# Row variances of a 64 MB tensor: TensorE's share given to VectorE and ScalarE, in tiles of 16 columns

## The chip, the core and the metric

The kernel runs on one core of a Trainium2 chip. The metric is the device time of one execution in microseconds (us), the median of several runs. Profiles are of one execution each.

## What is computed

```python
# x: (32, 512, 1024) float32
mean_sq = np.mean(x**2, axis=-1)
sq_mean = np.mean(x, axis=-1)**2
return mean_sq - sq_mean          # (32, 512): the variance of each row
```

There are 16384 rows of 1024 numbers, 67.1 MB to read and 64 KB to write.

## The kernel before

The rows are laid out so that partition p holds rows 128p to 128p+127. A *column* i is one row on each of the 128 partitions: a 128x1024 block of 512 KB. There are 128 columns, and each needs its mean and its mean square.

Three ways of doing a column share the work:

- **bn** (`do_bn_col`, L109): VectorE reads the two halves of the row with `bn_stats` (L112) and joins them with `bn_aggr` (L115). That gives mean and variance at once.
- **Square with a sum** (`do_square_col`, L117): ScalarE squares the row and sums it (L118, an ACTIVATE followed by a read of the accumulator), which gives the mean square. The plain sum then comes from another place: a `reduce_sum` of VectorE (L171, L206), a Copy pass of ScalarE with a sum (L213), or TensorE.
- **TensorE sums** (`do_tensor_cols`, L126): eight transposes of 128x128 (L133) add up in PSUM, VectorE copies the folded block to SBUF (L142), a matmul with ones sums it (L143), and VectorE copies the sums out (L152).

The columns 0 to 103 are loaded in 13 tiles of 8 columns (32 KB per partition, 4 MB each, L165), in three buffers. In each tile three columns are bn columns, two are Square plus `reduce_sum`, three are Square plus TensorE. The eight columns 120 to 127 are loaded first of all (L79) into a buffer of their own, and one of them is done with each of the tiles 2 to 9. The columns 104 to 119 come last, in seven loads of 4, 4, 2, 2, 2, 1 and 1 columns (L195), into a buffer of 64 KB per partition that nothing else uses. They are done in a pattern of four: Square plus `reduce_sum`, Square plus Copy, bn, bn.

`combine` (L81) forms mean square less squared mean for the columns that are not bn columns: a small Square on ScalarE (L83) and a subtraction on VectorE (L90, L102). It is called for the first 64 columns, the eight early ones, and the next 40. The results of the columns 0 to 103 are stored from ScalarE's queue (L189), beside the last loads. At the end the last 24 columns are joined (L221, L230) and stored from SP's queue (L237).

All loads stand on SP's queue in program order. A load into a buffer that was used before waits on SP for the engines that read it. Each engine runs its instructions in program order. Every ACTIVATE waits for the one ahead of it on ScalarE, since all write the same scratch tile.

Of the kernel before, what the change touches and what calls it, by code (L numbers as in the profile page):

```python
# [3 lines left out]

# [4 lines left out]


# [1 line left out]
def kernel(  # L13
# [2 lines left out]
    x: bass.AP,  # L16
    out: bass.AP,
):
    nc = tc.nc
    P = nc.NUM_PARTITIONS  # L20
    FP32 = mybir.dt.float32

    xf = x.flatten_outer_dims()
    N, D = xf.shape
    assert N % P == 0
    ntiles = N // P
    DCH = D // P

    def col_range(c0, n):
        return dataclasses.replace(  # L30
            xf,
            offset=c0 * D,
            ap=[[ntiles * D, P], [D, n], [1, D]],
        )

    out_ji = dataclasses.replace(out, offset=0, ap=[[ntiles, P], [1, ntiles]])

    FMAX = nc.vector.BN_STATS_FMAX
    nsub = (D + FMAX - 1) // FMAX

    inv_sqrt_d = 1.0 / math.sqrt(D)

    NBODY = 13
    END0 = NBODY * 8
    FILL0 = 120

    end_plan = [
        (104, 4),
        (108, 4),
        (112, 2),  # L50
        (114, 2),
        (116, 2),
        (118, 1),
        (119, 1),
    ]

    xpool = ctx.enter_context(tc.tile_pool(name="xpool", bufs=3))
    spool = ctx.enter_context(tc.tile_pool(name="spool", bufs=8))
    fpool = ctx.enter_context(tc.tile_pool(name="fpool", bufs=4))
    scpool = ctx.enter_context(tc.tile_pool(name="scpool", bufs=2))  # L60
    opool = ctx.enter_context(tc.tile_pool(name="opool", bufs=1))
    ppool = ctx.enter_context(tc.tile_pool(name="ppool", bufs=5, space=bass.MemoryType.PSUM))
    pspool = ctx.enter_context(tc.tile_pool(name="pspool", bufs=2, space=bass.MemoryType.PSUM))

    ident = opool.tile([P, P], FP32)
    masks.make_identity(nc, ident)
    ones = opool.tile([P, 1], FP32)
    nc.gpsimd.memset(ones, 1.0)

    pair_stage = opool.tile([P, 2, ntiles], FP32)  # L70
    msq_stage = opool.tile([P, ntiles], FP32)
    sqm_stage = opool.tile([P, ntiles], FP32)

    scratch = scpool.tile([P, D], mybir.dt.bfloat16)

    xt_end = opool.tile([P, FILL0 - END0, D], FP32)
    xt_fill = opool.tile([P, ntiles - FILL0, D], FP32)

    nc.sync.dma_start(out=xt_fill, in_=col_range(FILL0, ntiles - FILL0))  # L79

    def combine(c0, ngrp, gsize, nbn):  # L81
        n = ngrp * gsize
        nc.scalar.activation(  # L83
            out=sqm_stage[:, c0 : c0 + n],
            in_=pair_stage[:, 0, c0 : c0 + n],
            func=mybir.ActivationFunctionType.Square,
            scale=1.0 / D,
        )
        if nbn == 0:
            nc.vector.tensor_tensor(  # L90
                out=pair_stage[:, 1, c0 : c0 + n],
                in0=msq_stage[:, c0 : c0 + n],
                in1=sqm_stage[:, c0 : c0 + n],
                op=mybir.AluOpType.subtract,
            )
        else:
            var_v = pair_stage[:, 1, c0 : c0 + n].rearrange(
                "p (g k) -> p g k", k=gsize
            )
            msq_v = msq_stage[:, c0 : c0 + n].rearrange("p (g k) -> p g k", k=gsize)  # L100
            sqm_v = sqm_stage[:, c0 : c0 + n].rearrange("p (g k) -> p g k", k=gsize)
            nc.vector.tensor_tensor(  # L102
                out=var_v[:, :, nbn:gsize],
                in0=msq_v[:, :, nbn:gsize],
                in1=sqm_v[:, :, nbn:gsize],
                op=mybir.AluOpType.subtract,
            )

    def do_bn_col(xcol, i):  # L109
        stats = spool.tile([P, nsub, 6], FP32, name="stats")  # L110
        for s in range(nsub):
            nc.vector.bn_stats(  # L112
                out=stats[:, s, :], in_=xcol[:, s * FMAX : (s + 1) * FMAX]
            )
        nc.vector.bn_aggr(out=pair_stage[:, :, i], in_=stats)  # L115

    def do_square_col(xcol, i):  # L117
        nc.scalar.activation(  # L118
            out=scratch,
            in_=xcol,  # L120
            func=mybir.ActivationFunctionType.Square,
            scale=inv_sqrt_d,
            accum_out=msq_stage[:, i : i + 1],
        )

    def do_tensor_cols(xt, cols):  # L126
        if not cols:
            return
        psum_s = pspool.tile([P, 8], FP32, name="psum_s")
        for slot, (k, i) in enumerate(cols):  # L130
            psum_f = ppool.tile([P, P], FP32, name="psum_f")
            for ch in range(DCH):
                nc.tensor.matmul(  # L133
                    out=psum_f,
                    lhsT=xt[:, k, ch * P : (ch + 1) * P],
                    rhs=ident,
                    is_transpose=True,
                    start=(ch == 0),
                    stop=(ch == DCH - 1),
                )  # L140
            folded = fpool.tile([P, P], FP32, name="folded")
            nc.vector.tensor_copy(out=folded, in_=psum_f)  # L142
            nc.tensor.matmul(  # L143
                out=psum_s[:, slot : slot + 1],
                lhsT=folded,
                rhs=ones,
                start=True,
                stop=True,
            )
        i0 = cols[0][1]  # L150
        nt = len(cols)
        nc.vector.tensor_copy(  # L152
            out=pair_stage[:, 0, i0 : i0 + nt], in_=psum_s[:, :nt]
        )

    def do_filler_col(j):
        i = FILL0 + j
        do_square_col(xt_fill[:, j, :], i)
        do_tensor_cols(xt_fill, [(j, i)])

    for gi in range(NBODY):
        c0 = gi * 8
        nbn, ncl = 3, 2
        xt = xpool.tile([P, 8, D], FP32, name="xt")
        nc.sync.dma_start(out=xt, in_=col_range(c0, 8))  # L165

        for k in range(nbn):
            do_bn_col(xt[:, k, :], c0 + k)
        for k in range(nbn, 8):
            do_square_col(xt[:, k, :], c0 + k)  # L170
        nc.vector.reduce_sum(  # L171
            out=pair_stage[:, 0, c0 + nbn : c0 + nbn + ncl],
            in_=xt[:, nbn : nbn + ncl, :],
            axis=mybir.AxisListType.X,
        )
        do_tensor_cols(
            xt, [(k, c0 + k) for k in range(nbn + ncl, 8)]
        )

        if 2 <= gi <= 9:  # L180
            do_filler_col(gi - 2)

        if gi == 7:
            combine(0, 8, 8, 3)
        elif gi == 10:
            combine(120, 1, 8, 0)
        elif gi == 12:
            combine(64, 5, 8, 3)
            nc.scalar.dma_start(  # L189
                out=out_ji[:, 0:END0], in_=pair_stage[:, 1, 0:END0]  # L190
            )

    for (c0, ncols) in end_plan:
        off = c0 - END0
        nc.sync.dma_start(  # L195
            out=xt_end[:, off : off + ncols, :], in_=col_range(c0, ncols)
        )
        for k in range(ncols):
            i = c0 + k
            mode = "CSAA"[(i - END0) % 4]  # L200
            xcol = xt_end[:, off + k, :]
            if mode == "A":
                do_bn_col(xcol, i)
            elif mode == "C":
                do_square_col(xcol, i)
                nc.vector.reduce_sum(  # L206
                    out=pair_stage[:, 0, i : i + 1],
                    in_=xcol,
                    axis=mybir.AxisListType.X,
                )  # L210
            else:
                do_square_col(xcol, i)
                nc.scalar.activation(  # L213
                    out=scratch,
                    in_=xcol,
                    func=mybir.ActivationFunctionType.Copy,
                    accum_out=pair_stage[:, 0, i : i + 1],
                )

    n_end = ntiles - END0  # L220
    nc.scalar.activation(  # L221
        out=sqm_stage[:, END0:ntiles],
        in_=pair_stage[:, 0, END0:ntiles],
        func=mybir.ActivationFunctionType.Square,
        scale=1.0 / D,
    )
    var_v = pair_stage[:, 1, END0:ntiles].rearrange("p (g k) -> p g k", k=4)
    msq_v = msq_stage[:, END0:ntiles].rearrange("p (g k) -> p g k", k=4)
    sqm_v = sqm_stage[:, END0:ntiles].rearrange("p (g k) -> p g k", k=4)
    nc.vector.tensor_tensor(  # L230
        out=var_v[:, :, 0:2],
        in0=msq_v[:, :, 0:2],
        in1=sqm_v[:, :, 0:2],
        op=mybir.AluOpType.subtract,
    )

    nc.sync.dma_start(  # L237
        out=out_ji[:, END0:ntiles], in_=pair_stage[:, 1, END0:ntiles]
    )


# [1 line left out]
_INS = ['x']  # L243
_OUTS = [((32, 512), 'float32')]


# [23 lines left out]
```

## Time and profile before

| What | Value |
|---|---|
| time, median of 3 runs | 167.7 us (167.53 to 167.71) |
| span of the profiled execution, first to last instruction | 165.9 us |
| VectorE (DVE) busy | 107.0 us (64%), 230 instructions |
| ScalarE (ACT) busy | 99.7 us (60%), 175 instructions |
| TensorE (PE) busy, matmuls | 82.8 us (50%), 470 instructions |
| loads on SP's queue (q1) | 67.12 MB, 94.7% of the 16 DMA engines' span |
| mean rate over the span | 405 GB/s |

The span is the time between the first and the last instruction of the profiled execution. The runs' times also take in what lies around it; the page gives no separate time for the profiled execution, so its span is set beside the median of the runs, 1.8 us above it.

A page of this profile cuts the span in 40 equal slices and gives each engine's busy share in tenths. The chain that ended last is followed back from the last instruction, at each step to what released it. A timeline line gives start, length, engine, line and operation.

### The profile page before, as it was taken

The numbers are of one execution on the slowest core, as the hardware profiler recorded it, in microseconds if no ns is written. First come the engines' busy times: TensorE is split into PE (matmuls) and PEld (weight loads), VectorE is DVE, ScalarE is ACT, GpSimd is POOL, SyncE is SP. The second block draws the span as 40 slices with busy tenths as digits, with TensorE's granted clock in tenths as the row PEclk, the third lists the DMA queues.
The fourth block names the chain that finished last, engine by engine and source line by source line (L and its number), as shares of the span: only waits on it lengthen the run. The fifth ranks groups of instructions, "written<-read, shape, count | busy, mean of one in ns | idle before, by whom it ended". The sixth has DMA issues, their size and how long they took to land.

```text
span 165.9 us, 1460 instructions
## 1 busy us (share of the span) xinstructions
PE 82.8 (50%) x470; PEld 78.6 (47%) x470; DVE 107.0 (64%) x230; ACT 99.7 (60%) x175; POOL 0.7 (0%) x7
## 2 busy tenths in 40 slices
PE   0000047293791957749497774929565391950000
PEld 0000046292780947749396764829464381930000
DVE  0000049295791967949396794939769393999993
ACT  3000049093790967939396694939767391998981
POOL 1000000000000000000000000000000000000000
PEclk9999999658576597865858598795978658585555
DMA  5999999999999999999999999999999999999930
GB/s 190 443 427 450 411 450 411 443 443 427 450 399 450 421 435 435 421 443 411 443 423 443 427 435 435 419 450 415 435 435 419 443 421 399 435 417 417 412 140 3
DMA packets 3320, 67.26 MB, mean 405 GB/s; under 512 B 625, under 2 KB 625, under 8 KB 881
## 3 DMA queue, kind: packets, MB, share of 16 engines
q1 hardware_dynamic: 3168, 67.12, 94.7%
q8 instruction: 3, 0.05, 0.1%
q10 hardware_dynamic: 144, 0.05, 0.1%
q14 instruction: 5, 0.03, 0.1%
HBM read 67.11 MB, written 0.07 MB: 405 GB/s over the span
## 4 chain that ended last, share of the span: by engine, by line
DMA 69%; DVE 28%; issue 0%; SPq 0%; ACT 0%; ACTq 0%
DMA xt<-in_x_dram 69%; DVE stats L112 16%; DVE pair_stage L171 7%; DVE pair_stage L206 3%; DVE pair_stage L115 2%; DVE folded L142 0%; SPq L79 0%; ACT sqm_stage L221 0%; SPq L165 0%; DVE pair_stage L230 0%; DVE pair_stage L102 0%; DVE pair_stage L152 0%; ACTq L221 0%
## 5 line engine op out<-in xcount | busy, mean ns | idle before, releaser
L118 ACT ACTIVATE scratch<-xt 128x1024 bf16<-128x1024 f32 x65 | 68.7, 1057 | 59.6 <-DMA xt<-in_x_dram 57.9
L133 PE MATMUL psum_f<-ident,xt 128*128 128x128 f32 x312 | 62.9, 392 | 53.9 <-DMA xt<-in_x_dram 53.9
L133 PEld LDWEIGHTS psum_f<-ident,xt 128*128 128x128 f32 x312 | 59.1, 212 | 54.9 <-DMA xt<-in_x_dram 31.8
L112 DVE BATCH_NORM_STATS2 stats<-xt 128x6 f32<-128x512 f32 x78 | 48.8, 667 | 50.5 <-DMA xt<-in_x_dram 50.5
L171 DVE TENSOR_REDUCE pair_stage<-xt 128x2 f32<-128x2048 f32 x13 | 29.5, 2270 | 0.0
L143 PEld LDWEIGHTS psum_s<-ones,folded 128*128 128x128 f32 x94 | 11.5, 191 | 14.6 <-DVE folded L142 14.6
L143 PE MATMUL psum_s<-ones,folded 128*128 128x1 f32 x94 | 12.5, 252 | 11.4 <-DVE folded L142 11.4
L118 ACT ACTIVATION_READ_ACCUMULATOR scratch<-xt 128x1 f32 x65 | 12.1, 186 | 0.0
L112 DVE BATCH_NORM_STATS2 stats<-xt_end 128x6 f32<-128x512 f32 x16 | 10.1, 666 | 0.0
L142 DVE COPY folded<-psum_f 128x128 f32<-128x128 f32 x47 | 9.8, 267 | 0.0
L115 DVE BATCH_NORM_AGGREGATE pair_stage<-stats 128x2 f32<-128x12 f32 x47 | 9.2, 197 | 0.1
L118 ACT ACTIVATE scratch<-xt_end 128x1024 bf16<-128x1024 f32 x8 | 8.5, 1056 | 1.1 <-DMA xt_end<-in_x_dram 0.9
L133 PE MATMUL psum_f<-ident,xt_fill 128*128 128x128 f32 x64 | 9.0, 286 | 0.0
L118 ACT ACTIVATE scratch<-xt_fill 128x1024 bf16<-128x1024 f32 x8 | 8.5, 1057 | 0.3
L133 PEld LDWEIGHTS psum_f<-ident,xt_fill 128*128 128x128 f32 x64 | 8.2, 155 | 0.0
L152 DVE COPY pair_stage<-psum_s 128x3 f32<-128x3 f32 (+1 forms) x21 | 3.3, 159 | 5.2 <-PE psum_s L143 4.7
L206 DVE TENSOR_REDUCE pair_stage<-xt_end 128x1 f32<-128x1024 f32 x4 | 4.7, 1185 | 0.0
L213 ACT ACTIVATE scratch<-xt_end 128x1024 bf16<-128x1024 f32 x4 | 4.2, 1056 | 0.1
L118 ACT ACT_TABLE_LOAD x1 | 1.3, 1283 | 0.7 <-PEq L254 0.7
L118 ACT ACTIVATION_READ_ACCUMULATOR scratch<-xt_end 128x1 f32 x8 | 1.5, 186 | 0.0
L118 ACT ACTIVATION_READ_ACCUMULATOR scratch<-xt_fill 128x1 f32 x8 | 1.5, 186 | 0.0
L83 ACT ACTIVATE sqm_stage<-pair_stage 128x64 f32<-128x64 f32 (+2 forms) x3 | 0.7, 228 | 0.7 <-DVE pair_stage L152 0.7
(12 smaller groups left out, 2.7 us busy)
## 6 DMA issues: line engine op xcount, KB each, us to landing
xt<-in_x_dram SPq DMA_DIRECT2D x13, 4096.0 KB, 23.1
xt_fill<-in_x_dram SPq DMA_DIRECT2D x1, 4096.0 KB, 12.6
xt_end<-in_x_dram SPq DMA_DIRECT2D x2, 2048.0 KB, 29.8
xt_end<-in_x_dram SPq DMA_DIRECT2D x3, 1024.0 KB, 36.1
xt_end<-in_x_dram SPq DMA_DIRECT2D x2, 512.0 KB, 24.1
out_dram<-pair_stage ACTq DMA_DIRECT2D x1, 52.0 KB, 6.8
out_dram<-pair_stage SPq DMA_DIRECT2D x1, 12.0 KB, 1.4
```

The lines of the kernel that those rows point to most:

```text
L83: nc.scalar.activation(out=sqm_stage[:, c0 : c0 + n], in_=pair_stage[:, 0, c0 : c0 + n], func=mybir.ActivationFunctionType.Square, scale=1 ...
L112: nc.vector.bn_stats(out=stats[:, s, :], in_=xcol[:, s * FMAX : (s + 1) * FMAX])
L115: nc.vector.bn_aggr(out=pair_stage[:, :, i], in_=stats)
L118: nc.scalar.activation(out=scratch, in_=xcol, func=mybir.ActivationFunctionType.Square, scale=inv_sqrt_d, accum_out=msq_stage[:, i : i + 1],)
L133: nc.tensor.matmul(out=psum_f, lhsT=xt[:, k, ch * P : (ch + 1) * P], rhs=ident, is_transpose=True, start=(ch == 0), stop=(ch == DCH - 1),)
L142: nc.vector.tensor_copy(out=folded, in_=psum_f)
L143: nc.tensor.matmul(out=psum_s[:, slot : slot + 1], lhsT=folded, rhs=ones, start=True, stop=True,)
L152: nc.vector.tensor_copy(out=pair_stage[:, 0, i0 : i0 + nt], in_=psum_s[:, :nt])
L171: nc.vector.reduce_sum(out=pair_stage[:, 0, c0 + nbn : c0 + nbn + ncl], in_=xt[:, nbn : nbn + ncl, :], axis=mybir.AxisListType.X,)
L206: nc.vector.reduce_sum(out=pair_stage[:, 0, i : i + 1], in_=xcol, axis=mybir.AxisListType.X,)
L213: nc.scalar.activation(out=scratch, in_=xcol, func=mybir.ActivationFunctionType.Copy, accum_out=pair_stage[:, 0, i : i + 1],)
```

## The change

TensorE, PSUM, `combine`, the early eight columns and the early store are dropped. The 128 columns are cut into eight tiles of 16 columns (64 KB per partition, 8 MB), in three buffers. A string for each tile says who does a column:

- **D**: a bn column on VectorE, two `bn_stats` (L53) and a `bn_aggr` (L56), as before.
- **A**: two passes of ScalarE. A Copy with a scale and a sum (L68) gives the negative mean times 1/sqrt(D) in `neg_mean`; a Square with a scale and `neg_mean` as its bias, with a sum (L76), gives the variance. Of the columns of one load, all Copy passes come ahead of all Square passes.

The tiles 0 to 5 are one load each, with 6 A and 10 D columns. Tile 6 is loaded in 10 and 6 columns, with 4 and 2 A columns among them. Tile 7 is loaded in 5, 3, 2, 1, 1, 1 and 1 columns, with 2, 1, 1, 0, 1, 0 and 1 A columns; its last two columns are loaded in halves of 512 numbers, each read by a `bn_stats` of its own. All loads stand on SP's queue (L34). One store of 64 KB (L105) on SP's queue ends the kernel.

```diff
-    NBODY = 13
-    END0 = NBODY * 8
-    FILL0 = 120
...
+    GROUP = 16
+    NGROUPS = ncols // GROUP
+    LOADS = [[GROUP]] * (NGROUPS - 2) + [[10, 6], [5, 3, 2, 1, 1, 1, 1]]
+    WHO = ["ADDADDADDADADDAD"] * (NGROUPS - 2) + ["ADDADDADADADDADD", "ADDADDADDADADA"]
...
+    def act_cols(cols):
+        s = D ** -0.5
+        for xcol, c in cols:
+            nc.scalar.activation(
+                out=junk,
+                in_=xcol,
+                func=ACTF.Copy,
+                scale=-s / D,
+                accum_out=neg_mean[:, c : c + 1],
+            )
+        for xcol, c in cols:
+            nc.scalar.activation(
+                out=junk,
+                in_=xcol,
+                func=ACTF.Square,
+                scale=s,
+                bias=neg_mean[:, c : c + 1],
+                accum_out=mv[:, 1, c : c + 1],
+            )
+    for g in range(NGROUPS):
+        c0 = g * GROUP
+        xt = xpool.tile([P, GROUP, D], FP32, name="xt")
+        k = 0
+        for n in LOADS[g]:
+            load(xt[:, k : k + n, :] if n > 1 else xt[:, k, :], c0 + k, n)
+            mine = range(k, k + n)
+            act_cols([(xt[:, j, :], c0 + j) for j in mine if WHO[g][j] == "A"])
+            for j in mine:
+                if WHO[g][j] == "D":
+                    dve_col(xt[:, j, :], c0 + j)
+            k += n
+        for j in range(k, GROUP):
+            stats = spool.tile([P, 2, 6], FP32, name="stats")
+            for h in range(2):
+                xh = xt[:, j, h * H : (h + 1) * H]
+                load(xh, c0 + j, 1, h * H, H)
+                dve_half(stats, h, xh)
+            dve_done(stats, c0 + j)
+    nc.sync.dma_start(
+        out=dataclasses.replace(out, offset=0, ap=[[ncols, P], [1, ncols]]),
+        in_=mv[:, 1, :],
+    )
```

More of the change, by code (lines that the diff above doesn't have):

```diff
@@ L2 @@
 import dataclasses
-import math
 from contextlib import ExitStack
@@ L7 @@
 import concourse.tile as tile
-from concourse import bass_utils, masks, mybir
+from concourse import mybir
 from concourse._compat import with_exitstack
@@ L21 @@
     FP32 = mybir.dt.float32
+    ACTF = mybir.ActivationFunctionType
     xf = x.flatten_outer_dims()
@@ L25 @@
     assert N % P == 0
[L26 to L33, printed above, removed]
-        )
[L36 to L41, printed above, removed]
-    NBODY = 13
-    END0 = NBODY * 8
-    FILL0 = 120
[L47 to L55, printed above, removed]
+    ncols = N // P
@@ L57, with load @@
+    H = D // 2
+    def load(dst, c0, n, f0=0, f=D):
+        ap = [[ncols * D, P], [D, n], [1, f]] if n > 1 else [[ncols * D, P], [1, f]]
+        nc.sync.dma_start(
+            out=dst, in_=dataclasses.replace(xf, offset=c0 * D + f0, ap=ap)
+        )
+    GROUP = 16
+    NGROUPS = ncols // GROUP
+    LOADS = [[GROUP]] * (NGROUPS - 2) + [[10, 6], [5, 3, 2, 1, 1, 1, 1]]
+    WHO = ["ADDADDADDADADDAD"] * (NGROUPS - 2) + ["ADDADDADADADDADD", "ADDADDADADDADA"]
     xpool = ctx.enter_context(tc.tile_pool(name="xpool", bufs=3))
@@ L58 @@
     spool = ctx.enter_context(tc.tile_pool(name="spool", bufs=8))
-    fpool = ctx.enter_context(tc.tile_pool(name="fpool", bufs=4))
-    scpool = ctx.enter_context(tc.tile_pool(name="scpool", bufs=2))
     opool = ctx.enter_context(tc.tile_pool(name="opool", bufs=1))
-    ppool = ctx.enter_context(tc.tile_pool(name="ppool", bufs=5, space=bass.MemoryType.PSUM))
-    pspool = ctx.enter_context(tc.tile_pool(name="pspool", bufs=2, space=bass.MemoryType.PSUM))
-    ident = opool.tile([P, P], FP32)
@@ L66 @@
[L66 to L94, printed above, removed]
-            )
-        else:
-            var_v = pair_stage[:, 1, c0 : c0 + n].rearrange(
-                "p (g k) -> p g k", k=gsize
-            )
[L100 to L235, printed above, removed]
+    mv = opool.tile([P, 2, ncols], FP32)
@@ new lines, with dve_half, dve_done, dve_col @@
+    neg_mean = opool.tile([P, ncols], FP32)
+    junk = opool.tile([P, D], mybir.dt.bfloat16)
+    def dve_half(stats, h, xh):
+        nc.vector.bn_stats(out=stats[:, h, :], in_=xh)
+    def dve_done(stats, c):
+        nc.vector.bn_aggr(out=mv[:, :, c], in_=stats)
+    def dve_col(xcol, c):
+        stats = spool.tile([P, 2, 6], FP32, name="stats")
+        dve_half(stats, 0, xcol[:, :H])
+        dve_half(stats, 1, xcol[:, H:])
+        dve_done(stats, c)
+    def act_cols(cols):
[7 more added lines that the diff above has]
+                accum_out=neg_mean[:, c : c + 1],
+            )
+        for xcol, c in cols:
[6 more added lines that the diff above has]
+                accum_out=mv[:, 1, c : c + 1],
+            )
@@ new lines @@
+    for g in range(NGROUPS):
[11 more added lines that the diff above has]
+        for j in range(k, GROUP):
+            stats = spool.tile([P, 2, 6], FP32, name="stats")
+            for h in range(2):
[3 more added lines that the diff above has]
+            dve_done(stats, c0 + j)
@@ L237 @@
     nc.sync.dma_start(
-        out=out_ji[:, END0:ntiles], in_=pair_stage[:, 1, END0:ntiles]
+        out=dataclasses.replace(out, offset=0, ap=[[ncols, P], [1, ncols]]),
+        in_=mv[:, 1, :],
     )
```

## The prediction

> **What bounds the kernel now.** I read the page's slices first, then the chain of work that ended last, then the timeline of the last 16 us, then stretches of the DMA.
>
> The slices (40 of 4.15 us) and the queues:
>
> ```profile
> ACT  3000049093790967939396694939767391998981
> ...
> DMA  5999999999999999999999999999999999999930
> ...
> q1 hardware_dynamic: 3168, 67.12, 94.7%
> q8 instruction: 3, 0.05, 0.1%
> ```
>
> The DMA row is full from the second slice to the 38th, while ScalarE (ACT) has gaps until slice 36. The stream of loads is the floor, and what follows its end is the tail. Queue q8 is the fetching of instructions: three packets.
>
> Pieces of the chain in order of time (start, length, what):
>
> ```profile
> 1.16 21.87 DMA xt<-in_x_dram
> ...
> 24.93 0.11 DVE pair_stage L115
> 25.04 1.15 DVE stats L112 x2
> 26.19 0.11 DVE pair_stage L115
> ...
> 29.19 24.30 DMA xt<-in_x_dram
> ...
> 59.63 22.99 DMA xt<-in_x_dram
> ...
> 88.77 23.06 DMA xt<-in_x_dram
> ...
> 117.98 23.04 DMA xt<-in_x_dram
> ```
>
> The first piece ends at 23.02 (its end from the next piece), when 16 columns are in SBUF. The others end at 53.49, 82.62, 111.83 and 141.02, 24 columns apart: 30.47, 29.13, 29.21 and 29.19 us. So 16 columns cost 19.42 to 19.47 us (431 GB/s), and one interval lost 1.3 us more than the rest. By the trace's DMA packets a 16 KB packet of q8 ran for 1.10 us from 49.08, and from the next landing on the last of the 16 DMA engines came 2.04 us after the first, not 0.75: the fetch held up the engine that was last anyway, and each tile waits for the last engine. VectorE (DVE) takes a bn column every 1.26 us (24.93 to 26.19).
>
> The end, from the timeline (start, length, engine, line):
>
> ```profile
> 152.08 1.06 ACT L118 ACTIVATE scratch<-xt_end 128x1024 bf16<-128x1024 f32 x1
> 153.04 0.19 ACT L118 ACTIVATION_READ_ACCUMULATOR scratch<-xt_end 128x1 f32 x1
> 153.26 1.06 ACT L213 ACTIVATE scratch<-xt_end 128x1024 bf16<-128x1024 f32 x1
> ...
> 154.44 1.06 ACT L118 ACTIVATE scratch<-xt_end 128x1024 bf16<-128x1024 f32 x1
> ...
> 163.36 0.17 DVE L230 TENSOR_TENSOR pair_stage<-msq_stage,sqm_stage 128x12 f32<-128x12 f32 x1 [0.35 <-ACT sqm_stage L221]
> 163.56 0.35 SPq L237 DMA_DIRECT2D out_dram<-pair_stage  x1
> ```
>
> One ScalarE pass over a column with its sum is ACTIVATE, then a read of the accumulator, then the next pass: 1.18 us from start to start (152.08, 153.26, 154.44), the same for Square (L118) and Copy (L213). The last load lands at 160.89 (the trace's landings), the store is issued at 163.56, the span ends at 165.87: 2.31 us for issue, landing and end.
>
> **The change, part by part.** Sums are made against the span of 165.9 us; the median of the runs, 167.7, is 1.8 us above it, and I carry that 1.8 over.
>
> *What goes at nothing.* TensorE's 470 matmuls with their weight loads, the 68 PSUM copies and the 17 reductions on VectorE all lie under the stream. The POOL setup (0.7 us) lies under the first load. None of it was on the path, so its removal gains nothing directly.
>
> *VectorE after.* 10 of 16 columns in each full tile are bn columns: 10 x 1.26 = 12.6 us against 19.45 us of loading. In the last two tiles VectorE waits for data, and after the last half column it has one bn_stats (0.6) and one aggregate (0.2): it ends about 0.9 us after the last landing. This is not the bound.
>
> *ScalarE after.* Each A column takes two passes. The Copy pass has immediate operands as now: 1.18. The Square pass reads its bias from neg_mean, a 128x1 operand. Every pass of before has immediates, so no row shows this cost. From below: nothing, if the read lies under the pass (1.18 stays). From above: another 0.19, what the 128x1 accumulator read takes as a whole. I take 0.09, since the nearest row is that 128x1 access too: it starts 0.10 before its ACTIVATE ends (153.04 against 153.14), so only 0.09 of its 0.19 lies bare. A column then costs 1.18 + 1.27 = 2.45 us. The wait of Square for its Copy is the wait for the previous pass that before's passes have already, so it is inside the 1.18.
>
> The Trainium skill ("ScalarE: Activation LUTs", What ACT_TABLE_LOAD costs) speaks against this part: each [128,1] pointer operand adds about 93 ns to an ACTIVATE; its price of 186 ns plus 0.833 ns per element for immediates gives 1039 ns here, where the trace has 1057. By it the column costs 2.45 us as well; no row of before shows a pointer bias.
>
> A full tile has 6 A columns: 6 x 2.45 = 14.7 us, under 19.45, so ScalarE waits for each of the tiles 0 to 5. From tile 5 on it doesn't: tile 5 has 6 A columns, tile 6 has 4 and 2, tile 7 has 2, 1, 1, 1, 1. That is 18 columns, 36 passes, 18 x 2.45 = 44.2 us from the landing of tile 5. The stream needs for the 32 columns behind it 2 x 19.45 = 38.9, with the packets of 13 small loads some 39.5. I followed it load by load: 10 columns land 12.2 us after tile 5, when ScalarE has 2.5 us to go; the next 6 at 19.5, 5.0 to go; the next 5 at 25.6, 3.9 to go; then the last four A columns arrive at 29, 32, 34 and 37, and ScalarE starts them at 34.4, 36.8, 39.3 and 41.7. It is late at every load, so nothing of the lag is made up, and ScalarE ends 4.7 us after the last landing. This is the step that decides: the tail is now ScalarE's, not VectorE's.
>
> *The stream.* Tile 5 completes 96 columns. If every 16 columns take 19.45, that is at 23.02 + 5 x 19.45 = 120.3; before, 96 columns were there at about 111.83 + 9.73 = 121.6. Between the two lies the 1.3 us loss. PE's program is gone, and with 940 of 1460 instructions it is most likely what q8's three packets held; 8 KB fetches on q14 for the other engines stay (0.3 us each in the trace). I take 0.4 back for those, and subtract 0.3 since 64 KB rows halve the packets per byte (a 4 KB row takes 159 ns, a 32 KB row 1214, so a packet has about 10 ns of its own): 120.4. The bounds are 120.0 (nothing lost) and 121.6 (as now).
>
> *Loads and slots.* Load g+3 waits for ScalarE to leave tile g, 14.7 us after its landing; two further loads of 19.45 are queued by then, so the stream has 24 us in hand. The SP queue issues in order: the half-column loads stand behind waits for landings of tile 6 and of the first pieces of tile 7, the last of these 7 us ahead of the end. None starves the stream, and I cost them at nothing; if that cover were gone, each would cost at most a load's latency.
>
> *The tail.* The ACTIVATE and TENSOR_TENSOR that joined the results (163.01 to 163.53) go: 0.5 gained, but only behind an engine that is later. The first store from ScalarE's queue goes (0.37 us of ScalarE's time). The one store carries 64 KB, not 12: 512 bytes in a packet for 96. I add 0.15 to the 2.31.
>
> Sum: 120.4 + 44.2 = 164.6 end of ScalarE; 0.05 to the store; 2.31 + 0.15 to the end: span 167.1, 1.2 above before. Time 167.7 + 1.2 = 168.9.
>
> The Trainium skill ("DMA: Bandwidth & Descriptors", Measured) asks for at least 1 MiB a DMA, and eight of the loads here are smaller, 3 MB in all; by its row of 6.15 us for 1 MB those would take 18 us or more instead of 7.3. In before's trace the last two loads, of 512 KB, landed 1.25 and 1.24 us after the one ahead, 420 GB/s, so in a full queue the rule's price isn't seen.
>
> **The rivals.**
>
> 1. *The bias read is hidden.* Passes stay at 1.18, 36 x 1.18 = 42.5; span 120.4 + 42.5 + 2.5 = 165.4, time 167.2, faster by 0.3%. With the stream at 121.6 it is 168.4, slower. For it: the accumulator read is half hidden already. Against: a pass's fixed part (1057 less the stream of 1024 elements) is engine time, and passes don't overlap across the wait.
>
> 2. *The bias costs 0.19.* 18 x 2.55 = 45.9: time 170.6. With the old stream, 171.8.
>
> 3. *The stream ends it, as now: faster.* If ScalarE kept up, the end would be the last landing, 159.9, plus 0.9, plus 2.5: span 163.3, time 165.1. It decides from the point where a pair of passes takes under 39.5/18 = 2.2 us. The 85 passes of before with their sums all run at 1.06 plus the accumulator, so nothing in the profile gives 2.2.
>
> 4. *The 8 MB tiles stream worse*, or the fetches hit the last engine as now: tile 5 at 121.6 instead of 120.4, time 170.1, slower.
>
> **How the numbers follow.** Forecast (0.55): 168.9, from 168.5 to 169.5, slower. Rival 1 (0.18): faster in 0.12, same in 0.06. Rival 2 (0.07) and rival 4 (0.10): slower. Rival 3 (0.10): faster. So faster by over 0.2% (about what a measurement here can tell from no change) 0.22, same 0.06, slower 0.72. The range from 167.0 to 170.5 leaves out rival 3 and the far ends of 2 and 4.
>
> **What would show it.** In the changed profile: L76 ACTIVATE at about 1150 ns against 1057 for L68; the chain ending on ScalarE lines from tile 5 on, without gaps on ScalarE after 120 us; the store waiting for ScalarE about 4 us after DMA's end; VectorE done before it; q8 gone. I am wrong if L76 is no longer than L68, if ScalarE has idle gaps in the last 40 us, or if the third 8 MB landing isn't near 62 us.

## The result and the profile after

The changed kernel takes 168.97 us (168.92 to 169.04), the kernel before 167.69: 1.0078 times as long (95% interval 1.0064 to 1.0092). The profiled execution spans 167.2 us, the median lies 1.8 us above it, as before. (In the diff above, the two columns of tile 7's third load read D, A; the kernel has A, D. It is one of each either way.)

From the page of the changed kernel, the slices, the queues and the shares of the chain that ended last:

```profile
ACT  3000049990899609994499908996199999999993
...
DMA  7989997999799989989997998999799999999900
...
q1 hardware_dynamic: 2880, 67.18, 94.0%
q14 instruction: 4, 0.03, 0.0%
...
DMA 51%; ACT 39%; issue 5%; another core or an unknown queue 3%; SPq 0%; ACTq 0%
```

The shares of that chain in the kernel before:

```profile
DMA 69%; DVE 28%; issue 0%; SPq 0%; ACT 0%; ACTq 0%
```

The DMA row ends in the same slice as before. Its 7s, 8s and 9s alternate, but over the stretch from 23.0 to 100.7 us the DMA engines are busy all the time (share 1.00, 432 GB/s). q8 is gone. In the ACT row there is a dip every four to five slices up to slice 29 (ScalarE waits for a tile, 19.4 us) and none afterwards: ten nines and a part of the last slice, while DMA has ended two slices before the end. Before, the chain's second engine was DVE with 28%; now it is ACT with 39%.

The groups of ScalarE (in the columns: busy time, mean ns of one, idle time before them):

```profile
L76 ACT ACTIVATE junk<-xt,neg_mean 128x1024 bf16<-128x1024 f32 x48 | 55.1, 1148 | 1.5
L68 ACT ACTIVATE junk<-xt 128x1024 bf16<-128x1024 f32 x48 | 50.7, 1057 | 46.2 <-DMA xt<-in_x_dram 44.9
```

The Square with a bias from SBUF takes 91 ns more than the Copy with immediates. The Trainium skill's figure for such an operand ("ScalarE: Activation LUTs", What ACT_TABLE_LOAD costs), 93 ns, agrees with it.

The end, from the timeline of ScalarE and then of all engines:

```profile
120.37 1.06 ACT L68 ACTIVATE junk<-xt 128x1024 bf16<-128x1024 f32 x1 [4.66 <-DMA xt<-in_x_dram]
...
161.51 0.21 DVE L56 BATCH_NORM_AGGREGATE mv<-stats 128x2 f32<-128x12 f32 x1
...
163.26 1.15 ACT L76 ACTIVATE junk<-xt,neg_mean 128x1024 bf16<-128x1024 f32 x1
164.32 0.19 ACT L76 ACTIVATION_READ_ACCUMULATOR junk<-xt,neg_mean 128x1 f32 x1
164.53 0.35 SPq L105 DMA_DIRECT2D out_dram<-mv  x1
```

The bracket in the first line is the last one in ScalarE's timeline: after tile 5's landing no ACTIVATE waits for data again. The 36 passes run from 120.37 to 164.50. VectorE is done at 161.72, and the last load has landed at 160.65 (the trace's landings), so for the last 2.8 us the store waits for ScalarE alone.

### The profile page after: what moved, and what is told of

Read it like the earlier page. It is cut to its first block, busy times and chain, and to the rows that moved or that the text cites. A ratio compares the mean times of both kernels' runs of the same rounds, so it can differ in the third digit from the quotient of the medians.

```text
span 167.2 us, 517 instructions
## 1 busy us (share of the span) xinstructions
DVE 103.4 (62%) x240; ACT 116.0 (69%) x193; POOL 0.2 (0%) x4
## 4 chain that ended last, share of the span: by engine, by line
DMA 51%; ACT 39%; issue 5%; another core or an unknown queue 3%; SPq 0%; ACTq 0%
DMA xt<-in_x_dram 51%; ACT junk L68 21%; ACT junk L76 18%; SPq L34 0%; ACTq L134 0%; ACTq L68 0%
## 5 line engine op out<-in xcount | busy, mean ns | idle before, releaser
L53 DVE BATCH_NORM_STATS2 stats<-xt 128x6 f32<-128x512 f32 x160 | 99.1, 661 | 57.8 <-DMA xt<-in_x_dram 57.8
L68 ACT ACTIVATE junk<-xt 128x1024 bf16<-128x1024 f32 x48 | 50.7, 1057 | 46.2 <-DMA xt<-in_x_dram 44.9
L76 ACT ACTIVATE junk<-xt,neg_mean 128x1024 bf16<-128x1024 f32 x48 | 55.1, 1148 | 1.5
L56 DVE BATCH_NORM_AGGREGATE mv<-stats 128x2 f32<-128x12 f32 x80 | 15.7, 196 | 0.5
L76 ACT ACTIVATION_READ_ACCUMULATOR junk<-xt,neg_mean 128x1 f32 x48 | 9.0, 187 | 0.0
L68 ACT ACTIVATION_READ_ACCUMULATOR junk<-xt 128x1 f32 x48 | 8.9, 186 | 0.0
```

What stands on the lines that cost most here:

```text
L53: nc.vector.bn_stats(out=stats[:, h, :], in_=xh)
L56: nc.vector.bn_aggr(out=mv[:, :, c], in_=stats)
L68: nc.scalar.activation(out=junk, in_=xcol, func=ACTF.Copy, scale=-s / D, accum_out=neg_mean[:, c : c + 1],)
L76: nc.scalar.activation(out=junk, in_=xcol, func=ACTF.Square, scale=s, bias=neg_mean[:, c : c + 1], accum_out=mv[:, 1, c : c + 1],)
```

## The experiments

The theory: ScalarE has 18 two-pass columns behind the landing of tile 5, 44.1 us, where the stream needs 40.4; the difference sets the end. The main rival: the end is set by the stream and what stands behind it (the last loads, the one store), and ScalarE only happens to be busy. The times of the kernel before beside these runs were 167.6 to 167.8, and each run has its ratio to them.

### One price taken away: the bias from SBUF

```diff
                 scale=s,
-                bias=neg_mean[:, c : c + 1],
                 accum_out=mv[:, 1, c : c + 1],
```

> The Square pass gets an immediate bias of 0 in place of neg_mean; it leaves out the subtraction of the mean, so the A columns hold the mean square. Theory (ScalarE's 36 passes from tile 5 on set the end): the pass falls from 1148 to about 1057 ns, 18 of them stand in the last chain, ScalarE ends 1.65 us sooner (164.5 to 162.9), time 167.3. Rival (the stream, its small loads or the store sets the end, at a last landing of 160.65): 169.0, unchanged.

Measured: 167.21 us, 0.9964 of before (0.9951 to 0.9977), 1.76 less than the changed kernel. The group of the Square and the store in its profile:

```profile
L76 ACT ACTIVATE junk<-xt 128x1024 bf16<-128x1024 f32 x48 | 50.7, 1056 | 1.5
```

```profile
162.86 0.35 SPq L104 DMA_DIRECT2D out_dram<-mv  x1
```

The pass is 92 ns shorter, 18 of them make 1.66, and the store goes out 1.67 earlier (162.86 for 164.53). The last load lands at 160.65 in both kernels. The Square without the operand runs as fast as the Copy, so the 91 ns are the operand's. This one operand decides on which side of the kernel before the change ends.

### The same price doubled

```diff
-                func=ACTF.Copy,
+                func=ACTF.Identity,
                 scale=-s / D,
+                bias=zero,
```

> The Copy pass becomes an Identity pass with a 128x1 zero as bias, so that both passes read a pointer: the suspected cost doubled. Theory: 0.09 us more on each of 18 first passes in the last chain, ScalarE ends at 166.15, time 170.6. Rival (ScalarE not on the path): 169.0.

Measured: 170.46 us, 1.0156 of before (1.0131 to 1.0181). The two ScalarE groups, and the store:

```profile
L70 ACT ACTIVATE junk<-xt,zero 128x1024 bf16<-128x1024 f32 x48 | 55.1, 1148 | 20.7 <-DMA xt<-in_x_dram 19.3
L79 ACT ACTIVATE junk<-xt,neg_mean 128x1024 bf16<-128x1024 f32 x48 | 55.1, 1148 | 1.6
```

```profile
165.97 0.35 SPq L108 DMA_DIRECT2D out_dram<-mv  x1
```

Both passes now take 1148, and the store is 1.44 later than in the changed kernel; 18 x 0.091 is 1.64, less 0.24 since tile 5 is taken up at 120.13 here and not at 120.37. In both runs the time follows ScalarE's pass, and a stream or a store that set the end would have moved neither.

### One column moved off ScalarE

```diff
-    WHO = ["ADDADDADDADADDAD"] * (NGROUPS - 2) + [...
+    WHO = ["ADDADDADDADADDAD"] * (NGROUPS - 3) + ["ADDADDADDADADDDD", ...
```

> One A column of tile 5 becomes a D column, all else as in the changed kernel. Theory: ScalarE has one column of 2.45 us less in its last chain and ends near 162.05, VectorE ends near 161.9, time 166.5. Rival (the stream and the tail behind it): 169.0, or slightly more, since VectorE has 1.27 us more to do behind tile 5.

Measured: 166.42 us, 0.9914 of before (0.9890 to 0.9937). The end of its timeline:

```profile
158.62 1.31 DVE L53 BATCH_NORM_STATS2 stats<-xt 128x6 f32<-128x512 f32 x2 [0.41 <-DMA xt<-in_x_dram]
...
161.36 0.21 DVE L56 BATCH_NORM_AGGREGATE mv<-stats 128x2 f32<-128x12 f32 x1
161.71 0.19 ACT L76 ACTIVATION_READ_ACCUMULATOR junk<-xt,neg_mean 128x1 f32 x1
161.93 0.35 SPq L105 DMA_DIRECT2D out_dram<-mv  x1
```

ScalarE ends at 161.90 and VectorE at 161.57: level. One column of 128, 2.45 us of ScalarE's work, moves the store forward by 2.60 us (161.93 for 164.53); the other 0.15 is tile 5, taken up at 120.22 for 120.37. VectorE had the room: it still waits for one of the last loads (0.41 us, the first line).

### The tile's size alone

```diff
-    GROUP = 16
+    GROUP = 8
...
-    LOADS = [[GROUP]] * (NGROUPS - 2) + [[10, 6], [5, 3, 2, 1, 1, 1, 1]]
+    LOADS = [[GROUP]] * 12 + [[8], [2, 6], [5, 3], [2, 1, 1, 1, 1]]
...
-    xpool = ctx.enter_context(tc.tile_pool(name="xpool", bufs=3))
+    xpool = ctx.enter_context(tc.tile_pool(name="xpool", bufs=6))
```

> Tiles of 8 columns in six buffers (the same SBUF) in place of 16 in three; the same columns on the same engines, the 10-column load cut in 8 and 2. Theory: half of tile 5's ScalarE work is done before its second half lands, 7.4 us of the lag go, ScalarE keeps up and ends near 161.9 with VectorE; time 166.4. Rival 1 (it is the two passes, not the tile, that make ScalarE late): 169.0. Rival 2 (8 MB loads stream better than 4 MB): the last landing moves out by 0.3 to 0.5 and the time with it.

Measured: 166.38 us, 0.9911 of before (0.9888 to 0.9935). ScalarE's timeline has three brackets from 120 us on, of which the last two are here, then the end:

```profile
131.17 1.06 ACT L68 ACTIVATE junk<-xt 128x1024 bf16<-128x1024 f32 x1 [3.35 <-DMA xt<-in_x_dram]
...
147.05 1.06 ACT L68 ACTIVATE junk<-xt 128x1024 bf16<-128x1024 f32 x1 [1.19 <-DMA xt<-in_x_dram]
...
161.71 0.21 DVE L56 BATCH_NORM_AGGREGATE mv<-stats 128x2 f32<-128x12 f32 x1
161.99 0.35 SPq L105 DMA_DIRECT2D out_dram<-mv  x1
```

The store now waits for VectorE (161.92), since ScalarE is done at 161.75. ScalarE does exactly the same 96 passes at the same price, and yet waits for data as late as 147 us. With 16 columns in a tile all six A columns of tile 5 start when the 16th column is in; with 8, three of them are done by then. So it isn't the two passes by themselves that lose the time but the two passes on a tile that arrives in one piece. Column 96 lands 0.13 us later than in the changed kernel (120.41 for 120.28). That is no more than loads that are the same differ by from profile to profile: with tiles of 16 column 96 lands at 120.28, 120.28, 120.14 and 120.05 in the changed kernel and in three runs with the same loads up to there.

### TensorE's program, without its work

The changed kernel with 423 transposes of an identity tile into PSUM, which read no load and which nobody waits for:

```diff
+    masks.make_identity(nc, ident)
...
+    for i in range(47):
+        psum_f = ppool.tile([P, P], FP32, name="psum_f")
+        for ch in range(9):
+            nc.tensor.matmul(out=psum_f, lhsT=ident, rhs=ident,
+                is_transpose=True, start=(ch == 0), stop=(ch == 8))
```

> The changed kernel with a TensorE program beside it: 423 transposes of an identity tile into PSUM, which read no load and which nobody waits for. Theory (the 1.3 us that the stream lost in the kernel before came from fetching TensorE's program on one of the 16 DMA engines): queue q8 is back with three packets of 16 KB; where one of them hits the engine that is last anyway, all later landings move out by up to 1.3 us; tile 5 lands between 120.3 and 121.6 and the time is 169.0 to 170.3, ScalarE's lag behind tile 5 unchanged at 44.2 us. Rival (the earlier landing is due to the 64 KB rows alone): tile 5 at 120.3, 169.0.

Measured: 169.86 us, 1.0139 of before (1.0124 to 1.0155), 0.89 more than without the program (1.0078 of before). A queue of its page, and the last bracket of ScalarE and the store:

```profile
q8 instruction: 3, 0.05, 0.1%
```

```profile
121.24 1.06 ACT L82 ACTIVATE junk<-xt 128x1024 bf16<-128x1024 f32 x1 [4.66 <-DMA xt<-in_x_dram]
...
165.40 0.35 SPq L119 DMA_DIRECT2D out_dram<-mv  x1
```

The three packets are back (at 15.1, 29.7 and 44.3 us, 0.94 long, by the trace), tile 0 lands at 24.23 and not 22.99, its last DMA engine 1.99 us behind the first instead of 0.88. Tile 5 is 0.87 later, and the end with it. So 0.9 of the 1.3 us by which column 96 lands earlier than before come from the program that is gone. At the last load the two kernels are only 0.20 apart (160.85 for 160.65), but ScalarE's chain starts at tile 5, so the 0.87 there counts in full.

### The store behind the loads

Tiles of 8 columns, with the store of columns 0 to 111 issued on SP right behind the last load:

```diff
+    E = 112
+    for c, n in ((0, E), (E, ncols - E)):
         nc.sync.dma_start(
-            out=dataclasses.replace(out, offset=0, ap=[[ncols, P], [1, ncols]]),
-            in_=mv[:, 1, :],
+            out=dataclasses.replace(out, offset=c, ap=[[ncols, P], [1, n]]),
+            in_=mv[:, 1, c : c + n],
         )
```

> Tiles of 8 columns as in the run before, and the store cut in two on SP's queue behind the last load: columns 0 to 111 as soon as the last load is issued, 112 to 127 at the end. Theory: the first part runs on the DMA engines right behind the last load while ScalarE and VectorE finish; the final store carries 64 bytes a row for 512 and its issue to the span's end falls from 2.55 to some 2.3; time 166.1. Rivals: the 2.5 us are latency and don't depend on the bytes (166.4), or the first part holds up the last loads or the SP queue (167 or more).

Measured: 166.41 us, 0.9930 of before (0.9916 to 0.9943): no gain over tiles of 8 alone (166.38 us, 0.9911 of before). The final store:

```profile
162.12 0.34 SPq L107 DMA_DIRECT2D out_dram<-mv  x1
```

The span ends 2.51 us after that issue with 8 KB, and 2.52 us after it with 64 KB (tiles of 8 alone). The first rival holds: between 8 and 64 KB these microseconds do not depend on the bytes.

### VectorE's program, shortened

Tiles of 8 columns, with `bn_aggr` left out for the columns 0 to 95; one memset of zeros on VectorE stands ahead of everything for their results.

> Tiles of 8 columns as in the earlier run, without the 60 bn_aggr of the columns 0 to 95, so that those columns hold no result; VectorE's program is 180 instructions long in place of 240. In all runs so far an 8 KB packet of q14 runs 12.5 us after the landing of column 96 (6.8 us in the run with tiles of 8) whatever ScalarE does, about at VectorE's 180th instruction, and from the next landing on the last DMA engine is 1.0 us later. Theory (that packet is VectorE's program, and it is why the last load lands 1.0 us late): the packet is gone or comes after the last loads, the last load lands near 159.85 in place of 160.85, and the time falls from 166.4 to 165.4. Rival (the packet belongs to another engine, or the 1.0 us come from the smaller loads of the last tiles): last landing 160.85, 166.4.

Measured: 166.67 us, 0.9941 of before (0.9924 to 0.9957), and the last load lands at 161.16: the expected microsecond did not come. The packet did move, though. It runs at 153.92 in place of 127.21, both times when VectorE has run 181 or 182 instructions (by the trace). In all nine profiles one 8 KB packet runs at VectorE's 181st to 183rd recorded instruction and another at ScalarE's 190th to 194th; the latter is the one at 150.01 here. The load that lands at 140.88 with the full program lands at 140.21 here, its last DMA engine 1.28 behind the first and not 2.07; after the packets, at 156.02, it is 2.27. The first load behind column 96, of 8 columns, lands 9.72 us after it, where it took 10.68 with the full program. So the packet is part of VectorE's program and the late microsecond belongs to it; but a program of 180 instructions still fetches it before the loads end, and only its place was changed. The expectation says that the last DMA engine is 1.0 us later behind this packet in all runs so far; in the run with TensorE's program it is 0.29 us later (spread 2.11 before the packet, 2.40 behind it).

## Why the prediction was right, point by point

**The bias.** Costed at 0.09 between 0 and 0.19; measured 0.091. Taking it away moved the store by 18 times that, and giving the other pass one too moved ScalarE's 36 passes by as much. The reason was by analogy (the bare part of another 128x1 access, 0.09 us); no run shows that the two have the same cause, so the equality may be luck.

**ScalarE from tile 5 on.** 44.2 us expected (18 x 2.45 is 44.1), 44.1 measured, without a gap. That it is late at every load was followed load by load and holds. The prediction put the cause in the two passes and the number of A columns; the runs add that the tile of 16 columns is as much a cause, since the same passes in tiles of 8 keep up.

**The stream.** Tile 5 was expected at 120.4 and landed at 120.28; the third 8 MB landing, named at 62 us as a sign, came at 62.22. Of the terms, the lost fetch of TensorE's program was right in kind and worth 0.9. The 64 KB rows were put at 0.3: with tiles of 16 and no TensorE program column 96 lands at 120.05 to 120.28 (four profiles), with tiles of 8 at 120.41 to 120.71 (three), so tiles of 16 gave between 0.1 and 0.7. With that much scatter, it is partly luck that the sum of the terms came out to 0.1.

**The last landing.** This step was mis-sized: 39.5 us behind tile 5 were expected, 40.4 measured (160.65 for 159.9). The missing 0.9 are VectorE's 8 KB packet at 132.85, after which the spread of a landing over the DMA engines goes from 1.44 to 2.41 us; where that packet was moved, the delay moved with it (0.7 us there). The prediction had counted such packets for tile 5 and not behind it. It cost nothing, since ScalarE was later still: its lag was 3.85 us instead of 4.7.

**Small loads.** The four loads of 256 KB land 0.59 to 0.66 us apart, some 410 GB/s where the tiles of 8 MB come at 433 (19.35 us each). They were rightly costed at little. Leaving the Trainium skill's advice of 1 MiB or more ("DMA: Bandwidth & Descriptors", Measured) costs some 5% of the rate here, in a full queue.

**The tail.** From the store's issue to the span's end 2.46 were expected, 2.63 came. The 0.15 added for the store's bytes had the wrong reason, since with tiles of 8 a final store of 8 KB took 2.51 and one of 64 KB 2.52. Why the kernel before took 2.31 stays open. The tail was 0.17 longer than expected and ScalarE's end 0.1 earlier (164.50 for 164.6); that 168.9 met 168.97 rests on these two cancelling, which is luck.

**The rivals.** The hidden bias read would have given 167.2; the kernel in which it is gone runs in 167.21. The bias at 0.19 (second rival) and tile 5 at 121.6 (fourth) are ruled out by 0.091 and 120.28. The third rival, the stream as the end at 165.1, is not reached even where ScalarE keeps up: the runs with one A column less and with tiles of 8 take 166.4. Of the 1.3 they lack, 0.6 and 0.95 are the late last landing (160.49 and 160.85 for 159.9).

**What the prediction read wrongly of the kernel before.** It put VectorE's reductions and copies off the path. In the kernel before VectorE doesn't wait for a load any more after 141.05 and takes up the last column at 161.53, 0.64 us after it landed, and its four reductions of the last columns (L206) stand in that chain. At most those 0.64 us were there to gain, and since ScalarE ends later still, they don't show. ScalarE's last large gap is in slice 34, not 36, and the range to 170.5 leaves out rival 2 (170.6) whole. None of this bears on the sum.

## What to carry to other kernels

Where loads bound a kernel, look for the engine whose waits for data stop before the stream ends: from that landing on its work is a chain, and every one of its instructions is on the path. Large tiles make this worse, since an engine gets a whole tile's work when the tile's last byte lands; the work ahead of the end wants smaller pieces, or fewer columns on the slowest engine. Here either of the two, without a change to the passes, turns a loss of 0.8% into a gain of 0.9% (166.4 us), and both beat the kernel before.

## What was not expected of the hardware

Fetching a program can delay loads by more than the fetch itself takes. In the changed kernel an 8 KB packet takes 0.31 to 0.34 us, about what an 8 KB row of a load takes (0.31). Behind VectorE's, the last DMA engine of a landing is 1.0 us later (the spread goes from 1.44 to 2.41), and it doesn't catch up: the spread is 2.28 to 2.46 up to the last load. A tile waits for its last engine, so everything behind waits too. Why 0.3 us become 1.0 stays open.

But such delays do not add up, and not every packet costs something. Of the four 8 KB packets in the changed kernel, the one at 51.20 moved the spread by 0.55 us, and those at 68.16 and 157.22 by 0.05 or less. With TensorE's program beside it, where the spread was 2.11 already, VectorE's packet added 0.29; in the kernel before, where it was 2.19, it added nothing. So the last load lands at 160.65 in the changed kernel, at 160.85 with TensorE's program beside it, and at 160.89 in the kernel before. This fits packets that fall on different DMA engines, of which only the latest counts. The kept traces don't name the engine of a packet, so that is not shown.
